# Gate and up projections with the activations stationary and four of sixteen contraction tiles by seven products of sums

## The chip, the cores and the metric

The program runs on one core of one Trainium2 chip. The metric is the device time of one execution in microseconds, as the median of several runs. Before the change it is 2176.79 us (three runs, 2176.26 to 2177.47).

## The reference

The kernel computes a two-layer trunk over 256 tokens of width D = 2048: a convolution layer, a gated feed-forward (FFN), a shared K/V projection, a dilated attention layer, a second FFN, and a final norm. The change touches the first half of both FFNs:

```python
def _swiglu(h, w_gate, w_up, w_down):
    return (jax.nn.silu(h @ w_gate) * (h @ w_up)) @ w_down

h = h + _swiglu(_rmsnorm(h, ffn_norm_g[layer]), ffn_w_gate[layer], ffn_w_up[layer], ffn_w_down[layer])
```

Here `h` is 256 x 2048, `w_gate` and `w_up` are 2048 x 5632, `w_down` is 5632 x 2048, all float32.

## The kernel before

**Precision.** A float32 product is made of three products of parts. A weight block arrives by DMA as `raw` (128 partitions x 1024 numbers, 512 KB); ScalarE (ACT) copies it to `whi`, rounded to the matmul's input format, and VectorE (DVE) makes `wlo = raw - whi`. Activations are kept as two such parts in the tile `x` (or `hid`): `x[:, k, 0, :]` and `x[:, k, 1, :]` for contraction tile k of 128. The product is hi·hi + hi·lo + lo·hi.

**Gate and up (`project`, `group`, lines 302 and 327).** The weights are stationary: for each contraction tile and each 128 output columns, one matmul with 512 moving columns (`whi` against both parts of x, line 311) and one with 256 (`wlo` against the first part, line 315). The output is transposed already (features on partitions, tokens along the row), which is what the down projection needs as `hid`. A unit is 256 output columns: 4 blocks of gate, 4 of up, 22 units for each FFN. After each unit `collect` (line 404) adds the two halves of the PSUM bank, GpSimd (POOL) multiplies by the norm's factor `rstd` twice around the Silu, and ACT, DVE and POOL write the two parts of `hid` (lines 725 to 731).

**Down projection of the second FFN (`wd1`, lines 806 to 977).** It has the other layout already: the activations are stationary, a block is two contraction tiles x 512 columns, and `nat` (line 382) issues three matmuls with 512 moving columns for each contraction tile and each half t of the tokens. Its output has tokens on partitions, so the residual `hT` is turned over by 32 transposes first (`turn_over`, line 830). Two output column blocks are worked through together in a written order (`ITEMS`): "n" is a plain pair of contraction tiles, one block for each column block; "S" is a pair whose 2x2x2 products of blocks are made as seven products of sums instead of eight (`seven`, line 870). The sums of activations are made once by `sum_up`; the sums of weights are made for every S on DVE (`emit_sums`, line 202: four differences, then the split of seven half blocks), from weights that POOL's DMA queue loads (`load_sums`, line 187: one DMA of 512 KB and two of 256 KB). Four extra PSUM banks hold the products that go to more than one output; `combine` adds them.

**Order.** The weights come in one list, `blocks`. `next_block` emits the DMA (on SP's queue) and the splits up to two blocks ahead of the one used (`AHEAD`); there are three `raw` buffers and four of `whi` and `wlo`. `later(n, fn)` puts work n blocks on (`tick` after each block). Each engine executes its own instructions in order; the tile framework's scheduler sets that order.

```python
nc.tensor.matmul(bk[:, m, :, :], hi, x[:, k, :, :], ...)        # before, gate and up: 512 columns
nc.tensor.matmul(bk[:, m, 0, :], lo, x[:, k, 0, :], ...)        # and 256
nc.tensor.matmul(o, xs[0], hi, ...)                             # nat: three times 512
nc.tensor.matmul(o, xs[0], lo, ...)
nc.tensor.matmul(o, xs[1], hi, ...)
```

Of the kernel before, what the change touches and what calls it, by code (L numbers as in the profile page):

```python
# [16 lines left out]
P = 128  # L17
# [24 lines left out]
ITEMS = "n" * 8 + "Snn" * 3 + "Sn" + "nnn", "nnn" + "SnnSnSn" * 2 + "Sn" + "nnn"  # L42

# [41 lines left out]
def trunk(ctx: ExitStack, tc: tile.TileContext, xT, vec, const, w1, w2, wk, wv, wq, wo, wg0, wu0, wd0, wg1, wu1, wd1, fing, out):  # L85
# [39 lines left out]
    blocks = []  # L125

    def plan(w, u, kt_n, gk=GK):
        blocks.extend((w, u, g, gk) for g in range(kt_n // gk))

# [8 lines left out]
    for wg, wu, wd in ((wg0, wu0, wd0), (wg1, wu1, wd1)):  # L138
        for u in range(FT // 2):
            plan(wg, u, DT)  # L140
            plan(wu, u, DT)
        if wd is wd1:
            for half, items in enumerate(ITEMS):
                n_sums = items.count("S")
                sums, plain = iter(range(n_sums)), iter(range(n_sums, FT // GKV))
                ahead = [next(plain) for _ in range(2)]
                blocks.extend((wd, 2 * half + i, u, GKV) for i in range(2) for u in ahead)
                assert items.startswith("nn")
                for k in items[2:-3]:
                    if k == "S":  # L150
                        u = next(sums)
                        blocks.extend(("sums", half, u, q) for q in range(4))
                    else:
                        u = next(plain)
                        blocks.extend((wd, 2 * half + i, u, GKV) for i in range(2))
                rest = list(plain)
                assert len(rest) == 3 and next(sums, None) is None
                blocks.extend((wd, 2 * half + i, u, GKV) for i in range(2) for u in rest)
# [13 lines left out]
    halves = []  # L172
# [11 lines left out]

    all_sums = [(half, u) for half, items in enumerate(ITEMS) for u in range(items.count("S"))]

    def load_sums(n):

        if n < len(all_sums):
            half, u = all_sums[n]  # L190
            src = [wd1[2 * half + i, u].rearrange("p (k n) -> p k n", k=GKV) for i in range(2)]
            nc.gpsimd.dma_start(cst.rearrange("p (k n) -> p k n", k=GKV), src[0])
            for i in range(2):
                nc.gpsimd.dma_start(halves[i], src[1][:, i, :])
# [7 lines left out]
    def emit_sums(half, u, q):  # L202

        hi, lo = (wp.tile([P, GKV, NBV], F32R, name=n, bufs=AHEAD + 2) for n in ("whi", "wlo"))
        b12, b22 = halves
        if q == 0:
            first_raw[:] = [cst.rearrange("p (k n) -> p k n", k=GKV)]
# [22 lines left out]
        else:  # L230
            parts(0, first_raw[4])
            parts(1, first_raw[3])
            load_sums(all_sums.index((half, u)) + 1)
        ready.append((None, hi, lo))

    def emit_block():
# [4 lines left out]
        w, u, g, gk = blocks[i]  # L241
        shape = [P, gk, GK * NB // gk]
# [12 lines left out]
        for s in range(0, gk, step):  # L255
# [5 lines left out]
            if w is wd1:  # L261
                split(hi, lo, raw)
                continue
# [8 lines left out]
    def next_block(w, u, g, ahead=AHEAD):  # L272
        i = used[0]
        used[0] += 1
        assert blocks[i][:3] == (w, u, g) or (w == "sums" and blocks[i] == (w, *u, g))
# [146 lines left out]
    class Norm:  # L422
# [26 lines left out]
        def rstd_nat(self):  # L449

            st = aux([P, 2])
# [263 lines left out]

    silu = []

    def ffn_hidden(ff, wg, wu, x, norm):
        hid = new_x(ff, "hid", FT)
        for u in range(FT // 2):  # L720
            if u == 0:
                later(1, norm.rstd)
# [3 lines left out]
            silu.append(nc.scalar.activation(t, t, AF.Silu).ins)  # L726
            nc.gpsimd.tensor_tensor(out=t, in0=t, in1=_bc(norm.r, 2), op=ALU.mult)
            o = collect(project(wu, u, DT, x), ff, "t", 4)
            nc.vector.tensor_tensor(out=o, in0=o, in1=t, op=ALU.mult)
            nc.scalar.copy(hid[:, 2 * u:2 * u + 2, 0, :], o)  # L730
            nc.gpsimd.tensor_tensor(out=hid[:, 2 * u:2 * u + 2, 1, :], in0=o, in1=hid[:, 2 * u:2 * u + 2, 0, :].bitcast(F32),  # L731
                                    op=ALU.subtract)
        return hid

    with tc.tile_pool(name="ff", bufs=1) as ff:
        x, norm = out_proj(wd0, FT, ffn_hidden(ff, wg0, wu0, x, norm), None, "kv_g")
# [69 lines left out]
    with tc.tile_pool(name="ff", bufs=1) as ff:  # L806
        hid = ffn_hidden(ff, wg1, wu1, x, norm)
        table(AF.Sqrt, silu[-1])

        def plain_banks():  # L810

            b = [aux([P, NBV]) for _ in range(3)]
            return [b[0], b[2]], [b[1], one.tile([P, NBV], F32, name="b", tag="one")]

        def sum_banks():
            return [a[:, i, :, :].rearrange("p a b -> p (a b)") for a in (bank2(), bank2()) for i in range(2)]

        first = plain_banks(), sum_banks()
        ss = [little("ss", 8) for t in range(2)]
        buf = [ff.tile([P, 2, S], F32, name="t", bufs=4).rearrange("p a b -> p (a b)") for _ in range(4)]  # L820
        halves.extend(buf[0:2])
        gain = buf[2:4]

        def residual_of(c, t):
            return hT[:, 4 * c:4 * c + 4, t * P:(t + 1) * P]

        def wide(a):
            return a.rearrange("p (a b) -> p a b", b=P)
# [7 lines left out]
        n = 0  # L836
        for c in range(D // NBV):
            for t in range(2):
                later(n, lambda c=c, t=t, n=n: turn_over(c, t, first[1][n % 2 * 2]))
                n += 1  # L840
        later(n, lambda: load_sums(0))


        sums = rp.tile([P, SUMS, 4, 2, P], F32R, name="sums", tag="x")

        def sum_up(u):
            h, d = gain[0].rearrange("p (a b) -> p a b", b=S), wide(gain[1])
            two = hid[:, 2 * u:2 * u + 2, :, :].bitcast(F32)
            nc.vector.tensor_tensor(out=h, in0=two[:, :, 0, :], in1=two[:, :, 1, :], op=ALU.add)
            a11, a21, a12, a22 = (h[:, j, t * P:(t + 1) * P] for j in range(2) for t in range(2))  # L850
            for i, a, b, op in ((0, a21, a22, ALU.add), (1, d[:, 0, :], a11, ALU.subtract), (2, a11, a21, ALU.subtract),
                                (3, a12, d[:, 1, :], ALU.subtract)):
                nc.vector.tensor_tensor(out=d[:, i, :], in0=a, in1=b, op=op)
            nc.scalar.copy(sums[:, u, :, 0, :], d)
            nc.vector.tensor_tensor(out=sums[:, u, :, 1, :], in0=d, in1=sums[:, u, :, 0, :].bitcast(F32), op=ALU.subtract)

        for u in range(SUMS):
            later(2 + 3 * u, lambda u=u: sum_up(u))
# [10 lines left out]

        def seven(half, u, cs, ps, start):  # L870

            k = 2 * u
            two = [[sums[:, u, i, j, :] for j in range(2)] for i in range(4)]
# [151 lines left out]
```

## Time and profile before

| | |
|---|---|
| median of three runs | 2176.79 us |
| the profiled execution's own time | 2175.43 us |
| its span | 2173.7 us |
| stage gate and up, first FFN | 320.92 to 810.97 us |
| down projection, first FFN | 810.97 to 1055.50 us |
| stage gate and up, second FFN | 1439.51 to 1929.36 us |
| down projection, second FFN | 1929.36 to the end of PE's work at 2165.3 us |
| PE / DVE / ACT / POOL busy share of the span | 99% / 64% / 50% / 21% |
| HBM read, written | 398.28 MB, 2.10 MB |

The profile is one execution taken by the hardware profiler. An engine's busy time counts instructions only; matmuls overlap, so the duration of one (390 ns for 512 columns) is longer than the distance between the starts of two. A stage's length is read from the start of its first matmul to the start of the next stage's.

### The profile page before, as it was taken

Reading aid. Unit: us, or ns where it says so; the run is one execution under the profiler, and the core shown is the slowest. Engines: PE = TensorE matmul, PEld = TensorE weight load, DVE = VectorE, ACT = ScalarE, POOL = GpSimd, SP = SyncE. Lnnn points to the kernel's source line nnn. Section 1 sums busy time; section 2 is a strip of 40 time slices with the busy share of each in tenths; the row PEclk is TensorE's granted clock in tenths of the full one; section 3 lists DMA queues with packets and bytes.
Section 4 is the critical chain, followed back from the end, with each engine's and each line's share of the span. In section 5 each row is a group of like instructions: output and inputs, shape, how many; then the busy total and the mean of one; then the engine's idle time right before and its main releaser. Section 6 shows DMA issues by size and latency. Waiting matters only on the chain.

```text
span 2173.7 us, 31356 instructions
## 1 busy us (share of the span) xinstructions
PE 2153.9 (99%) x12221; PEld 1898.8 (87%) x12221; DVE 1399.7 (64%) x1776; ACT 1086.1 (50%) x1438; POOL 449.7 (21%) x327
## 2 busy tenths in 40 slices
PE   9999899999999999999999999999999999999998
PEld 8999788888888888888888888888888888888886
DVE  6888866555555554555545677665555555576877
ACT  6665545444444444444444566454444444454454
POOL 5998111112121210000000100011112121211311
PEclk9999999999999999999999999999999999999999
DMA  7444355555555555555565544555556555556664
GB/s 249 175 167 163 106 191 183 188 194 188 191 185 192 185 193 194 190 187 188 186 198 186 188 148 147 177 185 193 186 192 192 188 188 189 188 190 213 205 206 151
DMA packets 112821, 402.43 MB, mean 185 GB/s; under 512 B 12832, under 2 KB 13856, under 8 KB 112672
## 3 DMA queue, kind: packets, MB, share of 16 engines
q1 hardware_dynamic: 108288, 386.77, 54.1%
q0 software_dynamic: 3664, 12.59, 1.8%
q8 instruction: 95, 1.56, 0.3%
q10 hardware_dynamic: 720, 1.07, 0.1%
q14 instruction: 54, 0.44, 0.1%
HBM read 398.28 MB, written 2.10 MB: 184 GB/s over the span
## 4 chain that ended last, share of the span: by engine, by line
PE 97%; DVE 1%; DMA 1%; issue 0%; ACT 0%; POOL 0%; SPq 0%; DVEq 0%; ACTq 0%; POOLq 0%
PE pp L311 47%; PE pp L315 25%; PE pp L353 7%; PE aux L386 2%; PE aux L385 2%; PE aux L384 2%; PE pp L386 2%; PE pp L385 2%; PE pp L384 2%; PE b L386 1%; PE b L384 1%; PE b L385 1%; PE pp L378 1%; DMA raw<-w 0%; DVE aux L551 0%; PE pp L366 0%
## 5 line engine op out<-in xcount | busy, mean ns | idle before, releaser
L267 DVE TENSOR_TENSOR wlo<-raw,whi 128x1024 fp32r<-128x1024 f32 (+1 forms) x604 | 787.2, 1321 | 634.4 <-ACT whi L265 480.1
L265 ACT CAST whi<-raw 128x1024 fp32r<-128x1024 f32 (+1 forms) x649 | 678.4, 1047 | 812.7 <-PE pp L311 623.7
L311 PE MATMUL pp<-x,whi 128*128 128x512 f32 x3328 | 778.0, 390 | 0.0
L311 PEld LDWEIGHTS pp<-x,whi 128*128 128x128 f32 x3328 | 617.3, 188 | 123.3
L315 PEld LDWEIGHTS pp<-x,wlo 128*128 128x128 f32 x3328 | 414.2, 192 | 8.6
L315 PE MATMUL pp<-x,wlo 128*128 128x256 f32 x3328 | 418.6, 283 | 0.0
L311 PE MATMUL pp<-hid,whi 128*128 128x512 f32 x704 | 164.3, 390 | 0.0
L311 PEld LDWEIGHTS pp<-hid,whi 128*128 128x128 f32 x704 | 130.6, 188 | 26.1
L731 POOL TENSOR_TENSOR hid<-t,hid 128x512 fp32r<-128x512 f32 x44 | 57.9, 1315 | 408.1 <-ACT hid L730 408.1
L551 DVE SCALAR_TENSOR_TENSOR aux<-up,vecs,aux 128x256 f32<-128x256 f32 x350 | 140.9, 481 | 1.6 <-ACT aux L549 1.6
L436 POOL TENSOR_TENSOR sqacc<-sqacc,sq 128x512 f32<-128x512 f32 x22 | 29.5, 1342 | 516.5 <-ACT sq L432 506.3
L353 PE MATMUL pp<-x,whi 128*128 128x256 f32 x720 | 133.5, 287 | 0.0
L725 POOL TENSOR_TENSOR t<-t,rstd 128x512 f32<-128x512 f32 x44 | 57.1, 1298 | 344.3 <-DVE t L408 344.3
L353 PEld LDWEIGHTS pp<-x,whi 128*128 128x128 f32 x720 | 113.3, 192 | 0.9
L267 POOL TENSOR_TENSOR wlo<-raw,whi 128x1024 fp32r<-128x1024 f32 x45 | 107.2, 2409 | 21.5 <-ACT whi L265 21.5
L200 DVE TENSOR_TENSOR wlo<-raw,whi 128x1024 fp32r<-128x1024 f32 x66 | 87.6, 1360 | 29.2 <-ACT whi L198 28.4
L353 PE MATMUL pp<-x,wlo 128*128 128x256 f32 x360 | 101.8, 283 | 0.0
L407 ACT COPY t<-pp 128x512 f32<-128x512 f32 x104 | 61.2, 589 | 71.8 <-PE pp L311 71.8
L198 ACT CAST whi<-raw 128x1024 fp32r<-128x1024 f32 x66 | 68.3, 1051 | 52.7 <-DMA raw<-wd 35.4
L315 PEld LDWEIGHTS pp<-hid,wlo 128*128 128x128 f32 x704 | 87.6, 192 | 1.9
L315 PE MATMUL pp<-hid,wlo 128*128 128x256 f32 x704 | 88.2, 283 | 0.0
L384 PE MATMUL aux<-whi,hid 128*128 128x512 f32 x220 | 86.3, 392 | 0.0
(201 smaller groups left out, 2352.3 us busy)
## 6 DMA issues: line engine op xcount, KB each, us to landing
raw<-wg SPq DMA_DIRECT2D x176, 512.0 KB, 3.3
raw<-wu SPq DMA_DIRECT2D x176, 512.0 KB, 3.3
raw<-wd SPq DMA_DIRECT2D x154, 512.0 KB, 3.6
raw<-w SPq DMA_DIRECT2D x75, 512.0 KB, 3.3
raw<-wv SPq DMA_DIRECT2D x32, 512.0 KB, 4.2
raw<-wk SPq DMA_DIRECT2D x32, 512.0 KB, 3.7
raw<-wq SPq DMA_DIRECT2D x32, 512.0 KB, 3.2
raw<-wo SPq DMA_DIRECT2D x32, 512.0 KB, 3.3
```

Of the source, the lines that this page charges most:

```text
L198: made.append(nc.scalar.copy(hi, raw))
L200: made.append(nc.vector.tensor_tensor(out=lo, in0=raw, in1=hi.bitcast(F32), op=ALU.subtract))
L265: nc.scalar.copy(hi[:, part, :], raw[:, part, :])
L267: eng.tensor_tensor(out=lo[:, part, :], in0=raw[:, part, :], in1=hi[:, part, :].bitcast(F32), op=ALU.subtract)
L311: nc.tensor.matmul(bk[:, m, :, :], hi, x[:, k, :, :], start=k == 0, stop=k == kt_n - 1 and turned, skip_group_check=True)
L315: nc.tensor.matmul(bk[:, m, 0, :], lo, x[:, k, 0, :], start=False, stop=k == kt_n - 1 and not turned, skip_group_check=True)
L353: nc.tensor.matmul(bks[u][:, m, :], a[:, j, m * P:(m + 1) * P], b, start=kt == 0 and m == 0 and i == 0, stop=kt == DT - 1 and i == len(pas ...
L384: nc.tensor.matmul(o, xs[0], hi, start=start, stop=False, skip_group_check=True)
L385: nc.tensor.matmul(o, xs[0], lo, start=False, stop=False, skip_group_check=True)
L386: nc.tensor.matmul(o, xs[1], hi, start=False, stop=stop, skip_group_check=True)
L407: nc.scalar.copy(t, bk[:, :, 1, :])
L551: nc.vector.scalar_tensor_tensor(out=acc[i % 2], in0=win, scalar=w, in1=acc[i % 2], op0=ALU.mult, op1=ALU.add)
```

## The change

Gate and up of both FFNs take the layout of `wd1`: their weights are laid out in blocks of two contraction tiles x 512 columns, and gate and up of the same 512 columns (a chunk; 11 for each FFN) are the two column blocks that `two_blocks` works through together. The order of a chunk is "nnnnSnSn": six plain pairs and two S, so 4 of the 16 contraction tiles go by seven products; the first chunk has no S. After a chunk, `combine` and `hidden` make silu(gate) x up with tokens on partitions, and `turned`, six blocks into the next chunk, transposes the result (8 transposes) and writes the two parts of `hid`. The two sets of four PSUM banks change roles from chunk to chunk. POOL's three operations on each unit are gone.

The chunk's results and the weights for the sums need memory. The residual `hT` (2 MB) is therefore written to DRAM by one DMA on SP's queue (`keep`) early in each FFN, its place is used as `work`, and one DMA on POOL's queue brings it back (`residual_back`) in the down projection. In the second FFN the 32 transposes of `turn_over` move from the start of `wd1` into the first chunk, ahead of `keep`. `seven`, `sum_up` and `plain` become functions that both uses share.

```diff
+ITEMS_FF = "nnnnSnSn"
-        for u in range(FT // 2):
-            plan(wg, u, DT)
-            plan(wu, u, DT)
+        for c in range(F // NBV):
+            plan_two((wg, c), (wu, c), ff_items(c), ff_items(1).count("S"), 0)
...
+        def seven(k, start):
...
+            uses = (((ps[0], tokens(act, k0, 0), 0), (cs[0][0], tokens(act, k1, 0), 1)),
+                    ((cs[0][1], two[3], 1),),
+                    ((ps[1], two[0], 0), (ps[2], two[1], 1)),
+                    ((ps[3], two[2], 0), (cs[1][0], tokens(act, k1, 1), 1)))
...
-            bg = project(wg, u, DT, x)
-            t = collect(bg, ff, "t", 4)
-            nc.gpsimd.tensor_tensor(out=t, in0=t, in1=_bc(norm.r, 2), op=ALU.mult)
...
+        def keep():
+            nc.sync.dma_start(scratch, hT.rearrange("p a b -> p (a b)"))
+            work = rp.tile([P, 8, NBV], F32, name="work", tag="hT")
...
+        def combine(ps):
+            p1, p5, p6, p7 = ps
+            nc.scalar.copy(q[0][0], p1)
+            for o, p, i in ((q[0][1], p6, q[0][0]), (q[1][0], p7, q[0][1]), (q[1][1], p5, q[1][0]), (q[0][1], p5, q[0][1])):
+                nc.vector.tensor_tensor(out=o, in0=p, in1=i, op=ALU.add)
+        def hidden(c, cs, summed):
+            for t in range(2):
+                (g, u), r = q[t], norm.rn[:, t:t + 1]
+                if summed:
+                    nc.vector.tensor_tensor(out=g, in0=cs[t][0], in1=g, op=ALU.add)
+                silu.append(nc.scalar.activation(g, g if summed else cs[t][0], AF.Silu, scale=r).ins)
+                if summed:
+                    nc.vector.tensor_tensor(out=u, in0=cs[t][1], in1=u, op=ALU.add)
+                nc.vector.scalar_tensor_tensor(out=u, in0=u if summed else cs[t][1], scalar=r, in1=g, op0=ALU.mult, op1=ALU.mult)
+        def turned(c, cs):
...
+                        nc.tensor.transpose(b[:, a, t * P:(t + 1) * P], wide(q[t][1])[:, 2 * i + a, :], ident)
...
+                nc.scalar.copy(o[:, :, 0, :], b)
+                nc.vector.tensor_tensor(out=o[:, :, 1, :], in0=b, in1=o[:, :, 0, :].bitcast(F32), op=ALU.subtract)
+        for c in range(F // NBV):
...
+            hidden(c, cs, "S" in items)
+            later(5, lambda c=c, cs=cs: turned(c, cs))
...
+        nc.gpsimd.dma_start(hT.rearrange("p a b -> p (a b)"), scratch)
...
+        later(6, lambda: residual_back(scratch))
```

In the rows below, `L` numbers are lines of the kernel that the rows belong to (of the kernel before or of the changed one), a number behind a name tells one buffer from the next, and `xN` counts equal instructions in a row.

First TensorE. Before the change, at the start of the first FFN (z is the tile before it, x the FFN's input): a group of blocks is a run of matmuls with 512 moving columns and a run of as many with 256, turn and turn about, and the norm's sum (L443) stands once between.

```order
L311 MATMUL pp<-z,whi 128x512 x16
L311 MATMUL pp<-x,whi 128x512 x16
L315 MATMUL pp<-x,wlo 128x256 x16
L443 MATMUL aux<-sqacc,cst 128x256 x2
L315 MATMUL pp<-x,wlo 128x256 x16
L311 MATMUL pp<-x,whi 128x512 x32
L315 MATMUL pp<-x,wlo 128x256 x32
```

After the change, six blocks into the second chunk: the end of a plain block (`nat`, three matmuls of 512 columns), the eight transposes of the first chunk's result (`cst` holds the identity matrix, `aux` and `b` are two of the first chunk's banks), and the next plain block.

```order
L405 MATMUL pp_3794<-whi_3850,x_2831 128x512
L406 MATMUL pp_3794<-wlo_3851,x_2831 128x512
L407 MATMUL pp_3794<-whi_3850,x_2831 128x512
L869 MATMUL aux_3468<-cst_82,work_3515 128x128 x4
L869 MATMUL b_3470<-cst_82,work_3515 128x128 x4
L405 MATMUL pp_3793<-whi_3868,x_2831 128x512
L406 MATMUL pp_3793<-wlo_3869,x_2831 128x512
L407 MATMUL pp_3793<-whi_3868,x_2831 128x512
```

All matmuls of the stage now have 512 moving columns. Lines 405 to 407 hold 3 x (1336 + 160) = 4488 matmuls that read x or its sums, 384 of them in the `wv` stage as before; 4104 are left for gate and up, 2052 for each FFN, and each FFN has 88 transposes. Before, each had 1408 matmuls of 512 columns and 1408 of 256.

Second DVE. Before the change, in the middle of the stage (L267 is the split of a block, L408 the addition of `collect`, L729 the product of gate and up): four splits stand between the additions.

```order
L408 TENSOR_TENSOR t_4033<-pp_3944,t_4033 128x512
L729 TENSOR_TENSOR t_4033<-t_4033,t_3938 128x512
L267 TENSOR_TENSOR wlo_4048<-raw_4046,whi_4047 128x1024
L267 TENSOR_TENSOR wlo_4086<-raw_4084,whi_4085 128x1024
L267 TENSOR_TENSOR wlo_4092<-raw_4090,whi_4091 128x1024
L267 TENSOR_TENSOR wlo_4137<-raw_4135,whi_4136 128x1024
L408 TENSOR_TENSOR t_4128<-pp_4039,t_4128 128x512
```

After the change, over the end of the second chunk (L219 is the split of a block, L851 `combine`, L857 to L861 `hidden`; `work` holds the chunk's results, `aux` and `b` its sum banks, `pp` its own). The first row is the split of the chunk's last block, the next two splits are those of the third chunk's first two blocks, the last is that of its third block.

```order
L219 TENSOR_TENSOR wlo_4085<-raw_4083,whi_4084 128x1024
L851 TENSOR_TENSOR work_3515<-aux_3956,work_3515 128x512
L219 TENSOR_TENSOR wlo_4102<-raw_4100,whi_4101 128x1024
L851 TENSOR_TENSOR work_3515<-b_3958,work_3515 128x512
L851 TENSOR_TENSOR work_3515<-aux_3957,work_3515 128x512 x2
L219 TENSOR_TENSOR wlo_4120<-raw_4118,whi_4119 128x1024
L857 TENSOR_TENSOR work_3515<-pp_3793,work_3515 128x512
L860 TENSOR_TENSOR work_3515<-pp_3794,work_3515 128x512
L861 SCALAR_TENSOR_TENSOR work_3515<-work_3515,rstdn0_61 128x512 x2
L219 TENSOR_TENSOR wlo_4150<-raw_4148,whi_4149 128x1024
```

The pair L857, L860 stands there twice, once for each half of the tokens; the repetition is left out. Ten operations of `combine` and `hidden` now stand between the split of a chunk's last block and that of the next chunk's third, with two splits among them.

Third SP's queue of DMAs at the start of the first FFN. Before: loads of gate and up blocks and nothing else.

```order
L259 DMA raw_3403<-wg0 128x1024
L259 DMA raw_3409<-wg0 128x1024
L259 DMA raw_3464<-wg0 128x1024
L259 DMA raw_3470<-wg0 128x1024
L259 DMA raw_3514<-wu0 128x1024
```

After: the loads of blocks 0 to 6 of the first chunk, the store of the residual, and the loads of block 7 and on.

```order
L280 DMA raw_3403<-wg0 128x1024
L280 DMA raw_3409<-wg0 128x1024
L280 DMA raw_3471<-wu0 128x1024
L280 DMA raw_3489<-wu0 128x1024
L280 DMA raw_3516<-wg0 128x1024
L280 DMA raw_3534<-wu0 128x1024
L280 DMA raw_3561<-wg0 128x1024
L839 DMA residual_3464<-hT_84 128x4096
L280 DMA raw_3579<-wu0 128x1024
L280 DMA raw_3597<-wg0 128x1024
```

The store waits for the last write of `hT`, and every load behind it waits with it. In the second FFN 16 loads stand ahead of the store, and it waits for the last copy of `turn_over`.

More of the change, by code (lines that the diff above doesn't have):

```diff
@@ L138, in trunk @@
     for wg, wu, wd in ((wg0, wu0, wd0), (wg1, wu1, wd1)):
-        for u in range(FT // 2):
-            plan(wg, u, DT)
-            plan(wu, u, DT)
+        for c in range(F // NBV):
+            plan_two((wg, c), (wu, c), ff_items(c), ff_items(1).count("S"), 0)
         if wd is wd1:
             for half, items in enumerate(ITEMS):
[L144 to L158, printed above, removed]
+                plan_two((wd, 2 * half), (wd, 2 * half + 1), items, items.count("S"), 3)
         else:
```

253 lines of the change are left out of this document (152 added, 101 removed).

## The prediction

> **What bounds the kernel now.** I read the page first, then who waited for whom on TensorE, then the stages one by one.
>
> ```profile
> span 2173.7 us, 31356 instructions
> PE 2153.9 (99%) x12221; PEld 1898.8 (87%) x12221; DVE 1399.7 (64%) x1776; ACT 1086.1 (50%) x1438; POOL 449.7 (21%) x327
> PE 97%; DVE 1%; DMA 1%; issue 0%; ACT 0%; POOL 0%; SPq 0%; DVEq 0%; ACTq 0%; POOLq 0%
> PE pp L366 <- ACT cT L675: 4.9, 1, 4.9
> PE pp L353 <- DMA rawn<-w: 4.2, 1, 4.2
> PE st L621 <- DVE cT L592: 1.0, 1, 1.0
> ```
>
> TensorE (PE) works 2153.9 of 2173.7 us, the chain of waits that ends last is PE for 97%, and its three longest waits are 10.1 us in all, none in an FFN. So the time is the number of matmuls times the distance between their starts, and a change pays only through fewer or shorter matmuls, as long as no other engine makes PE wait. The four rows below are stages: length, then busy time of PE, weight loads, DVE, ACT, POOL, the granted clock, the DMA share and GB/s. The first two are gate and up of the two FFNs, the other two lie in the second down projection, which has the new layout with seven products already.
>
> ```profile
> 320.92:810.97 490.05, 490.05 (x2822) 433.92 (x2820) 287.16 (x247) 233.52 (x268) 90.51 (x66) 1.00 0.58 190
> 1439.51:1929.36 489.85, 489.85 (x2821) 433.85 (x2820) 286.93 (x246) 234.93 (x270) 90.50 (x66) 1.00 0.59 190
> 1956.00:2040.00 84.00, 84.00 (x373) 69.55 (x372) 61.68 (x75) 40.63 (x50) 13.22 (x17) 1.00 0.61 205
> 2040.00:2165.00 125.00, 125.00 (x553) 103.44 (x551) 105.95 (x135) 61.19 (x77) 27.24 (x29) 1.00 0.55 182
> ```
>
> PE is busy throughout all four, at the full clock. In the last, DVE works 85% of the time (105.95 of 125.00) and PE still never waits: that is the nearest picture of what gate and up become.
>
> **The new matmuls.** Two rows of the timeline of the down projection, with an S, two plain blocks and another S between them, lie 99 matmuls apart:
>
> ```profile
> 2074.67 0.39 PE L384 MATMUL b<-whi,hid 128*128 128x512 f32 x1
> 2097.11 0.39 PE L384 MATMUL aux<-whi,hid 128*128 128x512 f32 x1
> ```
>
> (2097.11 - 2074.67) / 99 = 0.2267 us each, plain or in an S. The order shows 2052 such matmuls for each FFN (11 chunks x 16 tiles x 2 products x 2 halves of the tokens x 3 = 2112, less 3 for each of 20 S). 2052 x 0.2267 = 465.2 us. With 2112 it would be 478.8, against the 490 of now: a pair of now costs 490/1408 = 0.348 us, so 0.121 for 256 columns, more than half of 0.2267. Part of a matmul's cost is paid for each matmul; six of 512 columns replace four of 512 and four of 256.
>
> The page TensorE: Matmul & The Clock Gate of the Trainium skill (section Back-to-back issue gap) gives a distance of columns/2.4 + 2.5 ns, thus 215.8 ns for 512 columns, 109.2 for 256 and 55.8 for 128. By it the stage of now would last 1408 x 0.325 = 458 us and the saving of both FFNs would be about 18 us, an estimate, for a time of 2159. The trace speaks against it: 490 us, and 226.7 ns.
>
> **The transposes.** The second down projection turns the residual over by groups of four transposes, one group behind each block of 12 matmuls:
>
> ```profile
> 1932.09 0.60 PE L833 MATMUL pp<-cst,hT 128*128 128x128 f32 x4
> 1954.52 0.60 PE L833 MATMUL pp<-cst,hT 128*128 128x128 f32 x4
> ```
>
> Seven such rounds take 22.43 us, 3.204 each; 12 x 0.2267 = 2.720 of it are the block's, so four transposes cost 0.484 us, 0.12 each. Each FFN gets 88 new ones: 10.6 us. The 32 of the residual only move. The norm's factor comes from eight one-column matmuls now (L454), as at the start of `wv`:
>
> ```profile
> 1060.94 1.02 PE L443 MATMUL aux<-sqacc,cst 128*128 128x256 f32 x4
> 1061.80 0.95 PE L454 MATMUL aux<-cst,sqacc 128*128 128x1 f32 x8
> 1062.61 0.48 PE L384 MATMUL pp<-whi,x 128*128 128x512 f32 x1
> ```
>
> 0.8 to 1.0 us; I take 1.0. The 0.9 us of L443 leave with the 490.
>
> **Sum on PE.** 465.2 + 10.6 + 1.0 = 476.8 us for each FFN; it saves 13.25 and 13.05, together **26.3 us**. Seen by parts: fewer products 2 x 60 x 0.2267 = 27.2; the other form 2 x (490 - 478.8) = 22.3; transposes -21.1; norm -2.0. The transposes eat the form's gain, and what is left is the seven products. The profiled execution took 2175.43 us, thus 2149.1; it lies 1.4 us below the median, so **2150.5** against the median.
>
> **Does DVE still keep up?** Groups of DVE by form, the first five from the down projection's second part, the sixth from `wv`, where POOL is idle, then two of ACT from the down projection:
>
> ```profile
> L200 DVE TENSOR_TENSOR wlo<-raw,whi 128x1024 fp32r<-128x1024 f32 x32 | 44.5, 1429 | 11.9 <-ACT whi L198 11.9
> L200 DVE TENSOR_TENSOR wlo<-sq,whi 128x512 fp32r<-128x512 f32 x14 | 9.7, 690 | 6.4 <-ACT whi L198 6.4
> L216 DVE TENSOR_TENSOR sqacc<-t,sq 128x512 f32<-128x512 f32 x7 | 4.8, 692 | 0.2
> L868 DVE TENSOR_TENSOR hT<-pp,hT 128x512 f32<-128x512 f32 x3 | 2.0, 681 | 0.0
> L903 DVE SCALAR_TENSOR_TENSOR sq<-hT 128x512 f32<-128x512 f32 x6 | 3.9, 682 | 0.0
> L267 DVE TENSOR_TENSOR wlo<-raw,whi 128x1024 fp32r<-128x1024 f32 x29 | 35.5, 1225 | 40.8 <-ACT whi L265 40.8
> L198 ACT CAST whi<-raw 128x1024 fp32r<-128x1024 f32 x31 | 31.9, 1051 | 24.6 <-DMA raw<-wd 21.9 <-ACT whi L198 1.5 <-PE b L386 1.2
> L198 ACT CAST whi<-sq 128x512 fp32r<-128x512 f32 x14 | 8.7, 622 | 26.0 <-PE aux L386 15.0 <-PE b L386 6.3 <-issue 4.7
> ```
>
> A chunk with two S is 14 whole splits (12 plain, 2 in S) x 1.225 + 10 half splits x 0.690 + 8 differences x 0.692 + 12 operations of `combine`, `hidden` and `turned` x 0.68 = 37.8 us; PE needs 186 x 0.2267 + 0.96 = 43.1. So DVE is at 88%, and at 93% if a plain split takes 1.429. POOL's operations, beside which it was that long, are gone from the stage. ACT has 24 us of work for a chunk (14 x 1.05, 15 of half that size x 0.62) and is no bound.
>
> The tightest place is the seam. The ten operations in the order's DVE rows can start only when the second S is through, 24 matmuls (5.4 us) before the chunk ends. By then block 0 and 1 of the next chunk have still to be split, and block 2's split stands behind all ten; PE needs it 24 matmuls after the end. That is 10.9 us of room for 10 x 0.68 + 3 x 1.225 = 10.5 us. I take **nothing**: starts lie closer than durations (below, two rows of 0.69 and 0.69 are 0.60 apart). If the room is overrun, the cost is bounded by one split and one half-size operation, about 2 us, on each of 20 seams, 40 us; the nearest row is the 85% stage without a wait, so zero it is, and 0.5 to 0.8 us for the range.
>
> ```profile
> 2090.90 0.69 DVE L200 TENSOR_TENSOR wlo<-t,whi 128x512 fp32r<-128x512 f32 x1
> 2091.50 0.69 DVE L200 TENSOR_TENSOR wlo<-sq,whi 128x512 fp32r<-128x512 f32 x1
> 2083.51 0.39 PE L384 MATMUL aux<-whi,sums 128*128 128x512 f32 x1
> 2080.27 0.53 POOL L192 DMA_DIRECT2D cst<-wd  x1 [15.21 <-DVE sq L216]
> 2087.11 1.22 DVE L200 TENSOR_TENSOR wlo<-cst,whi 128x1024 fp32r<-128x1024 f32 x1
> t<-wd POOLq DMA_DIRECT2D x22, 256.0 KB, 4.3
> ```
>
> The last four show the loads of an S: issued at 2080.27 as soon as the S before has been read, 3.2 us before PE begins the second block of that S (2083.51), 3 x 0.53 us of issue, landed 4.3 us after the last issue, about 5.4 in all, and used at 2087.11. In a chunk the second S follows the first at the same distance, with the same two blocks between.
>
> **The residual's trips.** No store or load of 2 MB is in the trace; bounds come from these rows:
>
> ```profile
> 323.66 0.68 DVE L469 TENSOR_TENSOR hT<-pp,hT 128x512 f32<-128x512 f32 x1
> 10.00:20.00 10.00, 10.00 (x70) 9.51 (x69) 8.47 (x16) 9.06 (x19) 0.00 (x0) 1.00 0.96 339
> 810.70:1055.30 244.60, 244.60 (x1410) 216.58 (x1410) 128.69 (x119) 102.28 (x111) 9.99 (x7) 1.00 0.58 189
> raw<-wg SPq DMA_DIRECT2D x176, 512.0 KB, 3.3
> raw<-wd SPq DMA_DIRECT2D x154, 512.0 KB, 3.6
> out<-raw SPq DMA_DIRECT2D x4, 256.0 KB, 2.7
> ```
>
> The store can go at 324.3, when `hT` is last written. Behind it on SP wait the loads of block 7 and on. At 339 GB/s the 2.1 MB take 6.2 us and block 7 lands 1.5 + 3.3 us later, at 335.3. PE reaches block 7 at 320.9 + 7 x 2.72 + 1 = 340.9, and copy and split take 2.3: 3.3 us to spare. In the second FFN the store waits for the residual's last turned tile after block 9 and block 16 waits behind it; the same sum leaves about as much. So **nothing**; at half the rate (12.4 us) each store costs 2.9 us. The way back starts 6 blocks into the down projection (17.7 us with the transposes; a block there takes 244.6/88 = 2.78) and DVE needs it after 11 blocks (30.6). The weights take 190 GB/s meanwhile; with the 149 left it needs 14.1 + 2.5 us and is 3.7 us late, but the splits of the next blocks stand ahead of that addition on DVE and cover some 5.7 us (block 14 is needed at 38.9, less its split and the two additions). **Nothing** again; at half of that rate it would cost 12 us, once, since the second FFN needs the residual much later. A trip cannot gain time.
>
> **Rivals.**
>
> A. The seams. DVE overruns the room at each chunk's end by 0.5 to 0.8 us: 20 x 0.65 = 13 us, a time of 2163. For it: 10.5 of 10.9 us. Against it: the 85% stage.
>
> B. The trips. Both stores, or the way back, go at half the rate: 5.8 or 12 us, a time of 2156 or 2163; I put 2160. For it: no such transfer has been seen here. Against it: the loads at 339 GB/s.
>
> C. **Slower than before:** the weights of the second S come late. PE begins its second block 45 matmuls, 10.2 us, after that of the first S, and before it ACT's copy, the split, four differences and a half split need 5.7 us; with the 3.2 us above, 7.7 us are left from issue to landing. From there each microsecond costs 20 (20 chunks with a second S); the 26.3 us are eaten at 9.0 us, and at twice today's landing (10.8) the time is 2150.5 + 3.1 x 20 = 2213. For it: 40 such loads move to POOL's queue, which shares the DMA engines with the weights. Against it: the same spacing at full PE in the down projection, and 205 GB/s there against 339 possible. The page SBUF — State Buffer of the Trainium skill (section SBUF: two separate sides) warns that DVE can keep POOL from writing the descriptors of such loads, though only in modes that use both its ports. The trace shows no sign of it: issues of 0.53 us beside a DVE at 85%.
>
> D. The change does not do what it says: excluded by the order, which has the 2052 matmuls.
>
> **Chances.** Forecast (2147 to 2154) 0.64; A 0.18; B 0.12; C 0.06. I predict 2151. The range is 2147 (transposes at 0.11 us save 1.8, the norm at 0.8 saves 0.4, and the runs differ by about 1) to 2165 (A and B with their middle prices), leaving out C and A's upper end. A measurement of this kernel can tell about 0.2%, 4.4 us, from no change. Faster by more: 0.92; within: 0.02; slower: 0.06.
>
> **What would show it.** Each gate-and-up stage at 477 us with PE busy throughout (the second 3.9 longer by the residual's transposes, the down projection shorter by as much); matmuls 0.2267 apart; no row of PE waits from L405 on `wlo` L219 above a few us in total (A, C), nor from block 7, block 16 or unit 1 of the down projection (B). Wrong would be a distance above 0.23 us in the S, a lower granted clock, or PE waits at every seam.

## The result, and the profile after

The changed kernel takes 2153.27 us (median of four runs, 2152.95 to 2154.73), the kernel before 2176.53 us beside it (2175.86 to 2177.47): a ratio of 0.9894, with a 95% interval of 0.9877 to 0.9911. Predicted were 2151 us, with a range of 2147 to 2165. The profiled execution of after took 2153.45 us.

From the page of after: the span, the busy time of each engine, the chain of waits; then five of the rows of who waited for whom on TensorE (us in total, times, longest).

```profile
span 2151.7 us, 29292 instructions
PE 2128.3 (99%) x10877; PEld 1821.1 (85%) x10877; DVE 1584.4 (74%) x2236; ACT 1123.0 (52%) x1534; POOL 333.1 (15%) x317
PE 93%; DVE 3%; DMA 2%; ACT 1%; issue 1%; POOL 0%; SPq 0%; DVEq 0%; ACTq 0%; POOLq 0%
PE pp L387 <- ACT cT L696: 5.0, 1, 5.0
PE pp L374 <- DVE xf L524: 3.7, 1, 3.7
PE pp L475 <- POOL sqacc L457: 1.7, 2, 0.9
PE aux L406 <- DVE wlo L219: 0.8, 1, 0.8
PE pp L406 <- DVE wlo L219: 0.3, 1, 0.3
```

PE is as busy as before, with 1344 fewer matmul instructions. The two rows on `wlo` L219, which the prediction named as the sign of its rivals A and C, hold 1.1 us in the whole program. The row on `sqacc` is new; the prediction didn't have it.

The stages of gate and up (first and second FFN), and two chunks between two rounds of transposes; columns as before (length, busy PE, weight loads, DVE, ACT, POOL, clock, DMA share, GB/s):

```profile
322.58:798.87 476.29, 475.43 (x2142) 394.30 (x2140) 378.06 (x471) 251.14 (x315) 33.97 (x61) 1.00 0.62 199
1428.93:1910.14 481.21, 479.58 (x2173) 397.35 (x2172) 378.14 (x470) 254.46 (x322) 34.92 (x63) 1.00 0.61 196
427.58:513.72 86.14, 86.14 (x389) 71.49 (x388) 70.69 (x89) 45.86 (x58) 6.41 (x12) 1.00 0.62 196
```

A chunk lasts 43.07 us and PE never waits in it; DVE works 70.69 of 86.14 us, 82%.

Where the time went, each stage from the start of its first matmul to that of the next (profiled executions, us). The projection w2 and all that lies ahead of it is the first column; the last columns are the second down projection up to the last matmul and the tail after it.

| | to FFN 0 | gate/up 0 | down 0 | attention | gate/up 1 | down 1 | tail | span |
|---|---|---|---|---|---|---|---|---|
| before | 320.92 | 490.05 | 244.53 | 384.01 | 489.85 | 235.52 | 8.82 | 2173.7 |
| after | 322.58 | 476.29 | 245.39 | 384.67 | 481.21 | 233.32 | 8.24 | 2151.7 |
| difference | +1.66 | -13.76 | +0.86 | +0.66 | -8.64 | -2.20 | -0.58 | -22.0 |

The 32 transposes of the residual have moved from the last stage into gate/up 1 (32 x 0.12 = 3.84), and 8 of the 88 new transposes of each FFN lie in the down projection behind it. The +1.66 ahead of the first FFN is no part of the change: each engine has the same instructions in the same order there, and in the ten runs below that stage ends anywhere from 321.14 to 325.42 us.

Two details in rows of the timeline (start, length). First the norm's eight matmuls, then one round of eight transposes between matmuls:

```profile
327.79 0.39 PE L407 MATMUL aux<-whi,x 128*128 128x512 f32 x1
329.04 1.05 PE L475 MATMUL pp<-cst,sqacc 128*128 128x1 f32 x8 [0.86 <-POOL sqacc L457]
329.95 0.48 PE L405 MATMUL aux<-whi,x 128*128 128x512 f32 x1
427.58 1.03 PE L869 MATMUL pp<-cst,work 128*128 128x128 f32 x8
428.37 0.48 PE L405 MATMUL aux<-whi,x 128*128 128x512 f32 x1
428.68 0.40 PE L406 MATMUL aux<-wlo,x 128*128 128x512 f32 x1
```

The norm costs 329.95 - 327.79 - 0.23 = 1.93 us instead of the 1.0 of the sum: 0.86 is a wait for POOL's sum of squares. The transposes cost 428.37 - 427.58 = 0.79, and 0.08 more on the next distance (0.31 instead of 0.23): 0.87, or 0.11 each.

The residual's trips, from the list of DMA issues (KB, median us from issue to landing):

```profile
residual<-hT SPq DMA_DIRECT2D x2, 2048.0 KB, 9.3
hT<-residual POOLq DMA_DIRECT2D x2, 2048.0 KB, 10.6
```

### The profile page after: what moved, and what is told of

Its sections match the earlier page's. It is cut to its first block, busy times and chain, and to the rows that moved or that the text cites. A ratio compares the mean times of both kernels' runs of the same rounds, so it can differ in the third digit from the quotient of the medians.

```text
span 2151.7 us, 29292 instructions
## 1 busy us (share of the span) xinstructions
PE 2128.3 (99%) x10877; PEld 1821.1 (85%) x10877; DVE 1584.4 (74%) x2236; ACT 1123.0 (52%) x1534; POOL 333.1 (15%) x317
## 4 chain that ended last, share of the span: by engine, by line
PE 93%; DVE 3%; DMA 2%; ACT 1%; issue 1%; POOL 0%; SPq 0%; DVEq 0%; ACTq 0%; POOLq 0%
PE pp L332 17%; PE pp L406 9%; PE pp L407 9%; PE pp L405 9%; PE pp L336 9%; PE pp L374 7%; PE aux L405 7%; PE aux L406 7%; PE aux L407 7%; PE b L407 2%; PE b L405 2%; PE b L406 2%; DVE aux L572 1%; DVE wlo L219 1%; DMA raw<-w 1%
## 5 line engine op out<-in xcount | busy, mean ns | idle before, releaser
L219 DVE TENSOR_TENSOR wlo<-raw,whi 128x1024 fp32r<-128x1024 f32 x338 | 410.7, 1237 | 169.4 <-ACT whi L217 168.1
L217 ACT CAST whi<-raw 128x1024 fp32r<-128x1024 f32 x338 | 349.2, 1051 | 312.3 <-DMA raw<-wu 89.8
L286 ACT CAST whi<-raw 128x1024 fp32r<-128x1024 f32 (+1 forms) x297 | 308.2, 1041 | 366.1 <-PE pp L332 185.9
L288 DVE TENSOR_TENSOR wlo<-raw,whi 128x1024 fp32r<-128x1024 f32 (+1 forms) x252 | 308.2, 1236 | 244.4 <-ACT whi L286 188.5
L405 PE MATMUL pp<-whi,x 128*128 128x512 f32 x668 | 260.9, 391 | 0.0
L407 PE MATMUL pp<-whi,x 128*128 128x512 f32 x668 | 260.0, 389 | 0.0
L406 PE MATMUL pp<-wlo,x 128*128 128x512 f32 x668 | 259.9, 389 | 0.0
L405 PE MATMUL aux<-whi,x 128*128 128x512 f32 x516 | 202.6, 393 | 0.0
L406 PE MATMUL aux<-wlo,x 128*128 128x512 f32 x516 | 201.0, 389 | 0.8 <-DVE wlo L219 0.8
L407 PE MATMUL aux<-whi,x 128*128 128x512 f32 x516 | 201.0, 389 | 0.0
L407 PEld LDWEIGHTS pp<-whi,x 128*128 128x128 f32 x668 | 125.4, 188 | 26.2
L405 PEld LDWEIGHTS pp<-whi,x 128*128 128x128 f32 x668 | 125.4, 188 | 25.6
L332 PE MATMUL pp<-x,whi 128*128 128x512 f32 x512 | 122.7, 393 | 0.0
```

The source lines that it names most:

```text
L217: made.append(nc.scalar.copy(hi, raw))
L219: made.append(nc.vector.tensor_tensor(out=lo, in0=raw, in1=hi.bitcast(F32), op=ALU.subtract))
L286: nc.scalar.copy(hi[:, part, :], raw[:, part, :])
L288: eng.tensor_tensor(out=lo[:, part, :], in0=raw[:, part, :], in1=hi[:, part, :].bitcast(F32), op=ALU.subtract)
L332: nc.tensor.matmul(bk[:, m, :, :], hi, x[:, k, :, :], start=k == 0, stop=k == kt_n - 1 and turned, skip_group_check=True)
L405: nc.tensor.matmul(o, xs[0], hi, start=start, stop=False, skip_group_check=True)
```

## Experiments

All are edits of the changed kernel, timed beside the kernel before. The ratios are to the kernel before, with their intervals.

**1. Without the seven products.**

```diff
-ITEMS_FF = "nnnnSnSn"
+ITEMS_FF = "nnnnnnnn"
...
-            if c == 0:
-                load_first_sums(wg, here)
```

> All eight pairs of every chunk are plain; form, transposes, norm and the residual's trips stay. Theory (TensorE is the bound, a matmul costs 0.2267 us whether plain or in an S, and what is left of the change is the seven products): 60 more matmuls in each FFN, 2 x 60 x 0.2267 = 27.2 us, so 2153.3 + 27.2 = 2180.5 us, slightly slower than the kernel before the change; stage of gate and up 13.6 us longer in each FFN. Rival 1 (an S pays less than its matmuls, because its half splits or the seam cost something): 2165 to 2175. Rival 2 (the form alone is the gain): 2153 or less.

2178.81 us, ratio 1.0011 (1.0002 to 1.0020). Its gate-and-up stages:

```profile
321.14:811.07 489.93, 488.99 (x2202) 405.56 (x2200) 247.81 (x235) 213.68 (x226) 1.80 (x1) 1.00 0.64 194
1441.32:1935.07 493.75, 492.88 (x2234) 408.69 (x2232) 249.69 (x240) 218.29 (x235) 2.85 (x3) 1.00 0.64 194
```

489.93 us against 490.05 before the change: the new form alone gains nothing, because the 80 transposes that lie in the stage and the norm's 1.93 us cost what it saves. Against the changed kernel the first stage is 13.64 us longer and the second 12.54 (13.5 without the changed kernel's one wait at a seam, 0.92 us); 60 x 0.2267 are 13.60. The medians lie 25.5 us apart. Both rivals fall: an S costs its matmuls, and nothing else that the stages show.

**2. Without the transposes of the result.**

```diff
-                for a in range(2):
-                    for t in range(2):
-                        nc.tensor.transpose(b[:, a, t * P:(t + 1) * P], ...)
```

> The 8 transposes of each chunk are left out, so hid is written from banks that hold no transposed result (the output is not the reference's). Theory: 176 transposes at 0.11 us (trace of the changed kernel) to 0.12 us (prediction) are 19.4 to 21.1 us on TensorE's path, so 2132 to 2134 us. Rival (they lie partly in time in which TensorE's next matmul would wait for weights anyhow): 2140 to 2153.

2139.45 us, ratio 0.9830 (0.9815 to 0.9845): 13.8 us less than the changed kernel, neither 19 nor nothing. The two stages of gate and up lose 8.78 and 9.47 us; that is 18.25 for 160 transposes, 0.114 each, as the theory says. But the two down projections, which lose eight transposes each, get longer, by 1.30 and 1.40 us. In the first of them, from the timeline of POOL, ACT and PE:

```profile
794.68 0.54 POOL L884 DMA_DIRECT2D hT<-residual  x1 [25.85 <-DVE work L861]
806.21 2.09 ACT L286 CAST whi<-raw 128x1024 fp32r<-128x1024 f32 x2 [7.78 <-DMA raw<-wd]
808.56 2.35 PE L336 MATMUL pp<-hid,wlo 128*128 128x256 f32 x16 [1.73 <-DVE wlo L288]
```

With no transposes to wait for, the way back of the residual starts 4.7 us into the stage (which begins at 790.02) instead of 18 (816.85 in the changed kernel). Three blocks of weights that are issued behind it land after 10.5, 10.5 and 8.7 us, where the two ahead of it took 3.6 and 3.5; ACT waits 7.78 us for a block, and PE 1.73. In the second down projection the way back starts 6.5 us into the stage, and PE waits 0.34 and 0.76 us for blocks behind it. So the trip has a price; in the first down projection of the changed kernel, where it starts late, PE loses nothing.

**3. The two S side by side.**

```diff
-ITEMS_FF = "nnnnSnSn"
+ITEMS_FF = "nnnnnSSn"
```

> The two S of a chunk stand directly behind each other (nnnnnSSn), as many matmuls as before. By the arithmetic of the prediction's rival C: the 24 matmuls between them (5.4 us) are gone, so of the 7.7 us of room from the issue of the second S's loads to their landing 2.3 us are left, against 5.4 us that they take: 3.1 us late in each of 20 chunks, 62 us, so 2215 us, with waits of about 3 us on the splits of the second S. Rival (the loads are not what ends last): within 5 us of 2153.

2175.44 us, ratio 0.9993 (0.9984 to 1.0003): 22 us more than the changed kernel, a third of what the arithmetic gave. The two stages are 9.08 and 8.08 us longer, 0.86 for each of 20 chunks. One seam between the two S:

```profile
437.13 0.54 POOL L206 DMA_DIRECT2D work<-wg  x1 [32.78 <-DVE sqacc L235]
441.79 1.57 ACT L217 CAST whi<-work 128x1024 fp32r<-128x1024 f32 x2 [0.22 <-PE aux L407]
442.87 1.23 DVE L219 TENSOR_TENSOR wlo<-work,whi 128x1024 fp32r<-128x1024 f32 x1 [0.50 <-ACT whi L217]
446.67 0.68 DVE L219 TENSOR_TENSOR wlo<-work,whi 128x512 fp32r<-128x512 f32 x1
446.30 0.39 PE L405 MATMUL aux<-whi,xsums 128*128 128x512 f32 x1
446.53 0.61 PE L405 MATMUL pp<-whi,xsums 128*128 128x512 f32 x2
447.41 0.50 PE L406 MATMUL aux<-wlo,xsums 128*128 128x512 f32 x1 [0.27 <-DVE wlo L219]
work<-wg POOLq DMA_DIRECT2D x40, 512.0 KB, 4.0
```

The loads are not what comes late. Issued at 437.13 and landed 4.0 us later, the first is there at 441.1; ACT's copy starts at 441.79, because ACT is busy with the last copies of the first S until 441.56 and then waits 0.22 us for PE to leave a buffer of `whi`. From there the split, four differences and a half split run on DVE without a gap until 447.35, and PE could have used that half split at 446.53: it is 0.82 us late. Two other matmuls are put in between (446.53), and the next ones start further apart, so PE loses some 0.65 us at this place. The work after the copy (5.6 us) was as predicted (5.7). Wrong were the landing, since the copy needs the first load alone (4.0, not 5.4), and the issue, 4.4 us ahead of the first S's second block (441.54) and not 3.2. The profiled execution was one of the slower of its ten (2179.47 us, 26.0 above the changed kernel's). Beside the 17.2 us of the two stages, 4.9 are in its first down projection: here too the last transposes come early, the way back starts 7.8 us into the stage, and PE waits 3.04 us for `wlo`. Attention and the second down projection are 2.0 us longer each; why was not followed.

**4. The norm a block later.** `later(1, lambda: norm.rstd_nat(bank2))` becomes `later(2, ...)`.

> The norm's eight one-column matmuls come one block later. In the trace of the changed kernel they wait 0.9 us for POOL's square sums in each FFN. If that wait is on the path: 2 x 0.9 = 1.8 us less, so 2151.5 us, and no row of matmuls that wait for POOL's sqacc in the FFNs. Rival (the wait only takes the place of one for the next block's split): 2153.3 us.

2151.00 us, ratio 0.9885 (0.9870 to 0.9900). The row on `sqacc` is gone, and the stages are 475.35 and 480.32 us: 0.94 and 0.89 less. The wait was on the path. Of the medians' difference of 2.3 us the stages account for 1.8; the intervals of this run and of the changed kernel overlap, so it is the stages that show it.

**5. The residual stored twice.** One more line behind the store in `keep`, to another place in DRAM:

```diff
             nc.sync.dma_start(scratch, hT.rearrange("p a b -> p (a b)"))
+            nc.sync.dma_start(kept.tile([P, DT * S], F32, name="again"), hT.rearrange("p a b -> p (a b)"))
```

> The residual is stored twice in each FFN, the second store right behind the first on SP's queue, to another place in DRAM. By the prediction's arithmetic a store has 3.3 us to spare and a second one takes 6.2 us more at 339 GB/s: about 2.9 us late in each FFN, 5.8 us, so 2159 us, with waits on the splits of block 7 in the first FFN and of block 16 in the second. Rival (the queue lets the weights pass beside the stores, or the buffers hide more): 2153 to 2154 us.

2155.46 us, ratio 0.9903 (0.9886 to 0.9919). The interval overlaps that of the changed kernel, so the trace has to decide. The profiled execution was the slowest of the four (2159.19 us): 1.87 us of its excess lie ahead of the first FFN, where the program is the same, and the stages of gate and up are 0.74 and 2.85 us longer. New waits stand at the two places that were named: 0.36 us more at block 7 of the first FFN, and at block 16 of the second:

```profile
1482.28 0.49 PE L405 MATMUL pp<-whi,x 128*128 128x512 f32 x1 [0.96 <-ACT whi L217]
1483.54 0.50 PE L406 MATMUL pp<-wlo,x 128*128 128x512 f32 x1 [0.34 <-DVE wlo L219]
again<-hT SPq DMA_DIRECT2D x2, 2048.0 KB, 13.6
```

About 1.9 us at the second, 2.3 in all instead of 5.8. The first store lands after 9.2 us in this run, the second, issued 0.4 us behind it, after 13.6: it adds 4.8 us and not 6.2. So one store hides, with a cover, by an estimate from these numbers, of some 4.4 us in the first FFN (4.8 less the new wait) and 2.9 in the second.

**6 and 7. More work for DVE at each seam**, the same addition of `combine` made three or seven times:

```diff
-            for o, p, i in ((q[0][1], p6, q[0][0]), ...
+            for o, p, i in (*[(q[0][1], p6, q[0][0])] * 3, ...
```

> The first addition of combine is made three times (the same numbers to the same place), so DVE has two more operations at the seam of each of 20 chunks. By the prediction's durations (10.5 us of 10.9) the room is overrun by about 1 us at each seam: 20 us, so 2173 us. By the distances of the starts in the changed kernel's trace (0.60 and 1.13 us instead of 0.68 and 1.23) the ten operations and three splits take 9.4 us, two more 1.2 us: within the room, 2153 us.

> The same with six more operations at each seam: 3.6 us by starts, 4.1 us by durations. By durations the room is overrun by 3.7 us: 74 us, so 2227 us. By starts it is overrun by 9.4 + 3.6 - 10.9 = 2.1 us: 42 us, so 2195 us, with a wait of about 2 us on wlo in each chunk. Rival (the blocks that are split ahead cover still more): under 2165 us.

With two more: 2158.30 us, ratio 0.9916 (0.9898 to 0.9934), but the stages of gate and up are 476.25 and 481.00 us, the same as without. So at the seams two operations more cost nothing, as the starts had it. The 5 us are in the down projections (+1.84 and +3.24): in the first, the way back starts 7.8 us into the stage again, and the list of waits has

```profile
PE pp L336 <- DVE wlo L288: 1.6, 1, 1.6
```

In the second it starts after 17.7 us, as in the changed kernel, and PE still waits 0.7 and 0.8 us for weights that were issued beside it, and 1.4 us once later. Why it does so here and not there stays open.

With six more: 2240.06 us, ratio 1.0285 (1.0266 to 1.0303). The size is near that of the pessimistic sum, but neither theory had the mechanism. PE's longest waits in that run, and one of them in the timeline:

```profile
PE pp L405 <- DVE work L851: 37.8, 9, 6.1
PE aux L405 <- DVE work L851: 16.1, 10, 2.9
455.73 0.39 PE L407 MATMUL b<-whi,x 128*128 128x512 f32 x1
460.26 0.76 PE L405 MATMUL pp<-whi,x 128*128 128x512 f32 x1 [4.14 <-DVE work L851]
460.83 0.63 PE L406 MATMUL pp<-wlo,x 128*128 128x512 f32 x1
461.25 0.63 PE L407 MATMUL pp<-whi,x 128*128 128x512 f32 x1
463.97 0.39 PE L405 MATMUL pp<-whi,x 128*128 128x512 f32 x1
464.20 0.39 PE L406 MATMUL pp<-wlo,x 128*128 128x512 f32 x1
```

PE doesn't wait for a split (`wlo`), it waits for the additions themselves (L851): the next chunk's first matmuls write the PSUM banks in which the extra products of this chunk stand until `combine` has read them. All seven equal additions read one of those banks. The scheduler also put three whole splits between them (they start at 454.59, 456.52 and 458.29), so the splits are early: that of the next chunk's third block is ready 9.9 us before PE uses it. The end of the additions:

```profile
459.44 1.41 DVE L851 TENSOR_TENSOR work<-pp,work 128x512 f32<-128x512 f32 x2
461.36 1.28 DVE L851 TENSOR_TENSOR work<-pp,work 128x512 f32<-128x512 f32 x2
```

The first addition at 459.44 is the seventh equal one, and PE goes on as soon as it is through (460.26). The other three read banks that the next chunk needs only 24 matmuls later, and PE does not wait for them. In the changed kernel there is ample room at this place:

```profile
449.07 0.68 DVE L851 TENSOR_TENSOR work<-pp,work 128x512 f32<-128x512 f32 x1
452.01 1.28 DVE L851 TENSOR_TENSOR work<-pp,work 128x512 f32<-128x512 f32 x2
454.31 0.39 PE L405 MATMUL pp<-whi,x 128*128 128x512 f32 x1
```

The bank that is needed first has been read at 449.75 and is written from 454.31: 4.6 us to spare. The banks of the last two additions have been read at 453.29 and are written from 459.75. With two operations more the last additions end at 455.34, after the next chunk's first matmul (454.30), and that matmul did not wait.

**8. Three S in a chunk.**

```diff
-SUMS_FF = 2
-ITEMS_FF = "nnnnSnSn"
+SUMS_FF = 3
+ITEMS_FF = "nnSnSnSn"
...
-            later(5, lambda c=c, cs=cs: turned(c, cs))
+            later(3, lambda c=c, cs=cs: turned(c, cs))
```

The lines left out put one of the four sums of activations into the tile of x. Without them (run three_sums) there is no time: a third full set of sums needs a pool of 100 KB in each partition, and 98.47 KB are left.

> Three S in each chunk but the first (nnSnSnSn), so 6 of 16 contraction tiles by seven products; one of the four sums of activations of each S goes to the place of the tile of x that an S does not read, for memory, and the transposes come two blocks earlier, since the extra banks are needed earlier. If TensorE stays the bound: 3 fewer matmuls in each of 20 chunks, 20 x 0.68 = 13.6 us, so 2139.7 us. DVE by the trace of the changed kernel: 35.3 us for a chunk, plus 5 half splits and 4 differences (9 x 0.6 to 0.69), less one whole split (1.2): 39.5 to 40.3 us of the 42.4 that TensorE needs. Rival (DVE cannot place that at the seams): waits on wlo of 0.5 to 2 us in each of 20 chunks, 2150 to 2180 us.

2149.41 us, ratio 0.9875 (0.9859 to 0.9890). Only 3.9 of 13.6 us, just below the rival's range; the stages take 476.17 and 475.98 us, so the gain is in the second FFN. A pair of chunks of the first, and the new row among PE's waits:

```profile
507.28:593.69 86.41, 85.41 (x383) 70.21 (x382) 78.92 (x105) 49.34 (x66) 9.58 (x19) 1.00 0.60 195
PE pp L405 <- DVE hid L877: 2.9, 8, 0.4
```

DVE needs 39.5 us for a chunk, as estimated, 91% of the time. PE waits for it twice in such a pair: at one of the seams for `wlo` (0.6 us at 587.3), and at the first S for a bank that still holds the transposed result (L877). In the second FFN only the latter is left.

**9 and 10. Three S, the norm later, and the transposes at two places.** Both with the edit of experiment 4; the second has `later(2, ...)` for `turned`.

> Three S as in three_of_four, and the norm's matmuls one block later as in norm_later: 2149.4 - 1.8 = 2147.6 us if the two do not meet.

> As three_norm, with the transposes after two blocks of the next chunk instead of three. In three_of_four the first S waited 8 times 0.4 us for DVE's split of the transposed result, since the extra banks are those in which it stands. If that is all, the waits go (8 x 0.5 = 4 us): 2143.5 us. Rival: DVE has not made the result by then (the ten operations at the seam end about 4.5 us after the chunk's end, two blocks are 5.4 us), and TensorE waits for it instead: 2148 us or more.

2146.02 us (ratio 0.9857, 0.9841 to 0.9874), and with the earlier transposes **2140.45 us (0.9835, 0.9820 to 0.9850)**, 12.8 us below the changed kernel; the intervals don't meet. Two chunks of the last:

```profile
676.89:761.67 84.78, 84.78 (x383) 70.39 (x382) 79.15 (x106) 49.30 (x66) 9.54 (x18) 1.00 0.62 200
```

42.39 us for a chunk, where 183 x 0.2267 and the 0.87 of the transposes make 42.36: PE is the bound again, with DVE at 93%. The L877 row is gone. Two waits at seams are left, both in the first FFN (1.0 and 0.3 us); the stages take 470.49 and 472.16 us.

## Why the prediction was right, point by point

**The bound and the distance: right.** PE is the bound before and after, and 0.2267 us holds for plain matmuls and for those in an S, over whole chunks (43.07 measured, 43.1 predicted). Experiment 1 confirms the 27.2 us for 120 fewer matmuls (13.64 and 13.5 measured) and the reading "the transposes eat the form's gain" (with the norm).

**The sum: 26.3 us forecast, 22.0 between the spans, 23.3 between the medians.** The sum less the eight transposes that fall into the next stage is 475.8 for each FFN, and 479.7 with the residual's transposes in the second; 476.29 and 481.21 were measured. The term that was mis-sized is the norm, taken at 1.0 us: 1.93 in each FFN. The price came from a row in which the sum of squares had been ready for some 2 us (POOL ended it at 1059.41, L454 starts at 1061.80), and the wait for POOL was missed; experiment 4 shows that moving it gives it back. The transposes were taken at 0.12 and are 0.11, which returns about 0.9 in each FFN. That these two misses all but cancel within a stage is luck. One wait of 0.92 us at a seam of the second FFN (1872 us) is the only trace of rivals A and C. The rest of the 4.3 us lies outside the changed stages: 1.66 ahead of them, which is spread between runs, and 0.8 net in attention, the second down projection and the tail, not settled further; attention alone takes between 384.6 and 386.7 us in the runs above.

**DVE keeps up: right, and the tightest place was named rightly.** 35.3 us for a chunk, not 37.8, because starts lie closer than durations (in the rows of experiment 7, from the changed kernel, an addition is 0.68 us long, and two that follow each other, of one row, are over after 1.28). "Nothing" at the seam was right but for one wait. Of the splits at a seam, block 2's is the one that comes nearest to PE: in the first FFN it is ready 0.3 to 2.0 us before PE's first matmul with it, and with two operations more (experiment 6) 0.3 to 0.5. So starts, not durations, gave the right room. The one wait for a split in the two stages is at this place, at the last seam of the second FFN:

```profile
1869.99 1.42 DVE L861 SCALAR_TENSOR_TENSOR work<-work,rstdn 128x512 f32<-128x512 f32 x2 [1.62 <-ACT work L858]
1871.32 3.49 DVE L219 TENSOR_TENSOR wlo<-raw,whi 128x1024 fp32r<-128x1024 f32 x3
1872.59 0.50 PE L406 MATMUL aux<-wlo,x 128*128 128x512 f32 x1 [0.76 <-DVE wlo L219]
```

ACT's Silu (L858) stood behind a copy that had waited for its weights, the last two of the ten operations waited for the Silu, and the split of block 2, the first of the three in the second row, stood behind them, as the prediction had it. Experiment 7 does not test this place: its six operations hold a PSUM bank, and the splits were put ahead of them.

**The trips: right in the sum, the way back for another reason.** The store hides, and its cover is near the predicted 3.3 us and at the predicted blocks (experiment 5). The way back lands in 9.3 to 11.9 us, not 16.6: the prediction let the weights keep their 190 GB/s, but they are delayed too (last section). Rival B's half rate was not seen. What was seen is a price of another kind: where the way back starts 5 to 8 us into the first down projection (experiments 2, 3, 6), PE waits 1.6 to 3.0 us, though it lands no later there (9.7 to 11.6 us). In the changed kernel it starts after 18 us. The prediction had argued with the splits that cover the addition; the weights queued beside the load are what comes late.

**Rival C (second S late, 2213): right in sign, too large.** Experiment 3 took 5.4 us of its room away and found 0.86 us late in each chunk instead of 3.1. The load was not last; ACT's copies, the `whi` buffers that they wait for, and DVE's chain behind them were.

## What to carry to other kernels

Where one engine is at 99%, count its instructions and multiply by the distance of starts read from the nearest stage: that gave the stages within 0.4%, and the rest of the work is to look for each new wait. Price a small operation at its new place, with the producer that stands ahead of it there, and not where it was measured. A second engine at 82% to 93% is no bound by itself; what decides is which split, buffer or bank PE waits for first at the seams, and in what order the scheduler puts that work, so look for both before adding to it.

## What the runs showed of the hardware that was not expected

A wait of PE can cost more than itself. In experiment 7, after waits of about 4 us, the next matmuls start 0.43 us apart for some 3 to 6 us, then 0.227 again (the rows 460.83 to 464.20), so that the wait of 4.14 us makes 6.0; most waits of 1.3 to 1.7 us are followed by one distance of 0.33 and nothing more. The granted clock is 0.50 in such a stretch, here behind the wait of 4.14 us and, in experiment 3, behind the wait of 3.04 us in the first down projection (columns as before; the clock is the third from the end):

```profile
460.30:463.60 3.30, 3.30 (x8) 2.62 (x9) 3.30 (x6) 1.05 (x2) 0.00 (x0) 0.50 0.64 240
831.20:834.50 3.30, 3.30 (x9) 2.54 (x8) 0.81 (x1) 0.61 (x1) 0.00 (x0) 0.50 0.94 340
```

The Trainium skill, page TensorE: Matmul & The Clock Gate, section Part 1: The HAM clock gate, says that the array's clock falls to half after an idle window of about 3.4 us and returns after a busy one. The ten waits of 3.8 to 6.1 us in and right behind the two stages of experiment 7 agree: the trace has half the clock for 3.4 or 6.8 us around the end of each. But of the ten shorter ones (1.28 to 2.93 us) one of 1.79 us was followed by such a stretch as well, as was that of 3.04 us in experiment 3, so in these runs a wait need not last 3.4 us to cost it.

In the changed kernel the stores and loads of 2 MB landed after 8.5 to 11.9 us. A load of 2 MB delays the weights that are issued behind it: while the first way back was under way, all DMA together moved 336 GB/s, and the block of weights issued 0.5 us behind it landed after 11.6 us, against a median of 4.2.

```profile
816.85:828.76 11.91, 11.91 (x72) 10.60 (x71) 4.13 (x5) 2.49 (x3) 0.54 (x1) 1.00 0.93 336
```

PE did not wait there. Where the way back was issued 5 to 8 us into that stage, PE did; what makes the later moment harmless was not tested by itself.
